# RWKV keys turned to time-major form by VectorE blocks and SBUF transfers instead of TensorE transposes

## The chip, the cores and the metric

The kernel runs on one core of one Trainium2 chip. The metric is device time in microseconds (us) of one execution, and lower is better. The time before is the median of 3 runs, 2657.88 us (2653.09 to 2657.88). Engines are named as the profile names them: PE (TensorE matmul), PEld (its weight loads), DVE (VectorE), ACT (ScalarE), POOL (GpSimd), SP (SyncE, which here only issues transfers).

## The reference

One decoder layer on 2048 tokens of width 1024: RMSNorm, one input projection, then two mixers side by side (HGRN2 with 4 heads of 128, RWKV-7 with 8 heads of 64), an output projection, and a ConvFFN. The part that this case touches is the RWKV-7 state:

```python
def step(S, inp):
    rt, wt, kt, vt, at, bt = inp
    sa = jnp.einsum('bhvk,bhk->bhv', S, at)
    S = S * wt[:, :, None, :] + sa[..., None] * bt[:, :, None, :] + vt[..., None] * kt[:, :, None, :]
    y = jnp.einsum('bhvk,bhk->bhv', S, rt)
    return S, y
```

The kernel computes it by chunks of 64 tokens. Within a chunk the dependence of the tokens on each other is a triangular system, solved on VectorE. What a chunk adds to the state is a sum over its 64 tokens of an outer product of `kt` (or `bt`) with a value row. On TensorE such a sum runs over partitions, so the keys must lie with time on the partitions, while the stage before makes them with the key channel on the partitions. Turning them is the work that the change moves.

## The kernel before

Phase 1 (to about 1327 us) holds the projections and both mixers; phase 2 (the rest) is the last output projection and the ConvFFN. Phase 1 is written as three generators: `dense` (the projection matmuls, lines 270 to 272, 8 steps of 3 matmuls for each column group), `rw_stream` and `hg_stream`. A loop takes one piece of each in turn and fills up with `dense` work. A scheduler then sets the order of each engine's instructions from that recorded program; each engine runs its own list strictly in order.

`rw_super` handles 512 tokens of four heads, and is run 8 times (8 stages below). Partitions hold two heads of 64 channels. Its steps, by line:

- L714 to L718: DVE writes `KB`, the scaled keys, [128 channels, 8 groups, 4, 64 tokens]. L730: PE multiplies `KB` with `AR` into score tiles; L733: DVE masks them into `M` (8 instructions of 128x512 a stage).
- L739 to L748: the 32x32 diagonal blocks of `M` go to DRAM (`Ed`, 4 transfers of 64 KB in runs of 128 bytes) and come back as `E` (2 transfers), with one system to a partition.
- L750 to L756: `KBT`, the keys with time on the partitions: 16 PE transposes of 128x128 into PSUM and 2 ACT copies of 128x1024. **This is what is changed.**
- L758 to L775: `RHS` and `UV`. `AT` is transposed (L763), `v` is centred and turned by a matmul (L768), ACT copies both out of PSUM; `UV` receives the values.
- L777 to L788: `lv`, matmuls that read `UV`; results go to `RHS`.
- L796 to L802: 31 elimination steps on DVE, two instructions each. L806 and L812: the result `TZ` is turned by DVE transposes in 32x32 blocks.
- L815 to L845: matmuls z, z2 and qus, which need `TZ` and `RHS`; L865 and L878: the state matmuls, the first readers of `KBT`.
- L897 to L937: the 8 chunk steps of the state, group norm, gate, and the store of the stage's output.

Buffers go by tags. `UV` shares its one buffer with `W` (the decay powers, dead by L716). `KBT` shares one with `ai`, and `RHS` takes the buffer of `KB`. PSUM tiles of `bank2()` have 2 buffers, so the two that the transposes take are handed from and to their neighbours.

All transfers of `rw_super` stand in SP's list; the weights of `dense` are fetched by POOL's list.

Of the kernel before, what the change touches and what calls it, by code (L numbers as in the profile page):

```python
# [11 lines left out]
AF = mybir.ActivationFunctionType  # L12
# [6 lines left out]
P = 128  # L19
# [48 lines left out]
def tile_layer(ctx, tc, consts, x, norm1_w, w_in, hg_lb_logits, hg_norm_w, rw_shift_mu, rw_w0, rw_w2,  # L68
# [4 lines left out]
    V, S, TE = nc.vector, nc.scalar, nc.tensor  # L73
    dma, store = nc.sync.dma_start, nc.gpsimd.dma_start
# [11 lines left out]
    ident = cp.tile([P, P], F32, name="ident")  # L86
# [27 lines left out]
    def act(out_, in_, func, **kw):  # L114

        want = tables.get(func)
        if want is not None and want != tab["now"]:
            pre = S.preload_act_table_set(want)
            for u_ in tab["uses"]:
                tc.add_manual_dep(pre.ins, u_.ins.name, NOSYNC, reason="table order")  # L120
            tab.update(now=want, pre=pre, uses=[])
        i_ = S.activation(out_, in_, func, **kw)  # L122
        if want is not None:
            tc.add_manual_dep(i_.ins, tab["pre"].ins.name, NOSYNC, reason="table order")
            tab["uses"].append(i_)
        return i_
# [13 lines left out]
    with tc.tile_pool(name="vp", bufs=1, reuse_waits="tile") as vp, tc.tile_pool(name="ps0", bufs=1, space=PSUM, reuse_waits="tile") as pools["ps"]:  # L140
        rows = vp.tile([P, P], F32, name="rows")
        V.memset(rows, 0.0)
        n = 0
# [130 lines left out]
    def phase1(c1):  # L274
# [372 lines left out]
        def rw_super(nb, s_):  # L647

            tl = stage[("tl", nb)]
            r, k, v = (stage.pop(("rkv", nb, s_, w)) for w in range(3))  # L650
# [3 lines left out]
            def tile_(tag, shape, name):  # L654
                return rp.tile([P] + shape, F32, tag=tag, name=name)

            def bank2():
                return ps.tile([P, 2, BLK], F32, tag="rw", name="rw", bufs=2)
# [5 lines left out]

            ai = tile_("KBT", [2, 2, BLK], "ai")
            a, iW = ai[:, 0], ai[:, 1]
# [9 lines left out]
            c, km, sq = mk_[:, 0], mk_[:, 1], mk_[:, 2]  # L676
# [37 lines left out]
            KB = tile_("KB", [8, 4, 64], "KB")  # L714
# [8 lines left out]
            for j in range(2):  # L723
                for u in U:
                    s1 = bank2()
                    for i in range(4):
                        b, e = 2 * j + i // 2, i % 2
# [20 lines left out]
                dma(E[f:P:2], Ed)  # L748

            KBT = tile_("KBT", [2, 8, P], "KBT")  # L750
            for u in U:
                tp = bank2()
                for i in range(8):
                    TE.transpose(tp[:, i // 4, (i % 4) * P:(i % 4 + 1) * P],
                                 KB[:, 4 * u + i // 2, (i % 2) * 2:(i % 2) * 2 + 2, :], ident)
                act(KBT[:, u], tp.rearrange("p j (c t) -> p (j c) t", t=P), AF.Copy)  # L756
            yield
            RHS = tile_("KB", [8, 2, P], "RHS")  # L758
            UV = tile_("UV", [8, 2, P], "UV")
            tp = bank2()  # L760
# [100 lines left out]
            for u in U:  # L861
                for ch in range(8):
                    b, e = ch // 2, ch % 2
                    for h in range(2):
                        TE.matmul(xp[h * 64:h * 64 + 64, u, ch * 64:ch * 64 + 64], KBT[:, u, ch, h * 64:h * 64 + 64],  # L865
                                  UV[:, 4 * u + b, e, h * 64:h * 64 + 64], start=ch == 0, stop=False,
                                  tile_position=(0, h * 64), skip_group_check=True)
            for u in U:
                Q, G = M[:, 0, u, :, :, 0:64], M[:, 1, u, :, :, 0:64]
                yg = bank2()  # L870
                for w in range(2):
                    for b in range(4):
                        for e in range(2):
                            rs_ = slice(er0(e), er0(e) + 64)
                            sl = w * 256 + b * 64
                            for h in range(2):
                                rhs = (M[rs_, e, u, b, h, 64:128] if w == 0
                                       else KBT[rs_, u, 2 * b + e, h * 64:h * 64 + 64])  # L878
                                TE.matmul(yg[h * 64:h * 64 + 64, e, sl:sl + 64], Q[rs_, b, h, :], rhs,
# [8 lines left out]
            for u in U:  # L888
                for ch in range(8):
                    b, e = ch // 2, ch % 2  # L890
# [6 lines left out]
            for ch in range(8):  # L897
                b, e = ch // 2, ch % 2
# [185 lines left out]
        def rw_stream():  # L1084
            for n in range(2 * NBLK):
                while ready["rw"] <= n:
                    yield None
                yield from rw_super(n // 2, n % 2)
# [53 lines left out]
    with ExitStack() as c2:  # L1142
# [36 lines left out]
        with tc.tile_pool(name="op", bufs=1, reuse_waits="tile") as op_:  # L1179
# [7 lines left out]
            b = NBLK - 1  # L1187
# [53 lines left out]
            for dh in range(2):  # L1241
                accs = [pst("wacc") for _ in range(4)]
                for n, k in enumerate((0, 1, 4, 5, 2, 3, 6, 7)):
# [22 lines left out]
                    for q in range(12):  # L1266
                        i, t_ = (q % 4, q // 4) if first else (q // 3, q % 3)
# [231 lines left out]
    with tc.tile_pool(name="dn", bufs=1, reuse_waits="tile") as dn:  # L1499
# [61 lines left out]
        for s_ in range(DS, N):  # L1561
            g, p, kk = steps[s_]
# [60 lines left out]
```

## Time and profile before

| what | value |
|---|---|
| median of 3 runs | 2657.88 us |
| the profiled execution's own time | 2662.58 us |
| its span, first to last instruction | 2660.8 us |
| granted TensorE clock over the span | 0.992 |
| PE / DVE / ACT / POOL busy | 2560.2 / 1952.9 / 1389.2 / 380.4 us |
| transfers | 510.59 MB, mean 192 GB/s |

The page gives busy time by engine, then a line of digits for each engine over 40 equal slices of the span (about 66.5 us each; 9 means 90% or more busy). Phase 1 is the first 20 slices. Windows are stretches of the span in which busy time is added up. A row of a line or a tile gives count and the shortest, median and longest duration in ns. A wait is an engine's idle time, put down to what ended it.

### The profile page before, as it was taken

The numbers are of one execution on the slowest core, as the hardware profiler recorded it, in microseconds if no ns is written. First come the engines' busy times: TensorE is split into PE (matmuls) and PEld (weight loads), VectorE is DVE, ScalarE is ACT, GpSimd is POOL, SyncE is SP. The second block draws the span as 40 slices with busy tenths as digits, with TensorE's granted clock in tenths as the row PEclk, the third lists the DMA queues.
The fourth block names the chain that finished last, engine by engine and source line by source line (L and its number), as shares of the span: only waits on it lengthen the run. The fifth ranks groups of instructions, "written<-read, shape, count | busy, mean of one in ns | idle before, by whom it ended". The sixth has DMA issues, their size and how long they took to land. (4 is left out here: it accounts for less than half of the span.)

```text
span 2660.8 us, 51050 instructions
## 1 busy us (share of the span) xinstructions
PE 2560.2 (96%) x19595; PEld 2061.2 (77%) x19595; DVE 1952.9 (73%) x3728; ACT 1389.2 (52%) x2274; POOL 380.4 (14%) x686
## 2 busy tenths in 40 slices
PE   7999999989999999999899999999999999999998
PEld 5777777766777777777678888887888887888887
DVE  4877667576567765767678789987998887766556
ACT  5566453545535555445456754456545544545444
POOL 6433222212222122222100000000000000000000
PEclk9999999999999999999999999999999999999999
DMA  8645443445643456744493468646763553998665
GB/s 303 204 165 170 158 143 120 130 148 203 199 143 126 156 196 199 276 131 136 154 309 113 143 204 266 233 154 225 245 203 131 166 189 127 327 320 286 197 191 186
DMA packets 312714, 510.59 MB, mean 192 GB/s; under 512 B 46879, under 2 KB 143509, under 8 KB 312469
## 3 DMA queue, kind: packets, MB, share of 16 engines
q1 hardware_dynamic: 257937, 328.99, 37.4%
q0 software_dynamic: 54464, 178.32, 20.4%
q8 instruction: 154, 2.52, 0.4%
q14 instruction: 91, 0.75, 0.1%
q10 hardware_dynamic: 68, 0.02, 0.0%
HBM read 372.99 MB, written 134.22 MB: 191 GB/s over the span
## 5 line engine op out<-in xcount | busy, mean ns | idle before, releaser
L270 PE MATMUL pj<-hh,wh 128*128 128x512 f32 x960 | 393.4, 410 | 6.2 <-ACT rkv L122 3.3
L271 PE MATMUL pj<-hl,wh 128*128 128x512 f32 x960 | 377.8, 394 | 1.3 <-issue 1.3
L272 PE MATMUL pj<-hh,wl 128*128 128x512 f32 x960 | 377.5, 393 | 0.0
L270 PE MATMUL ua<-Bh,uwh 128*128 128x512 f32 x704 | 276.4, 393 | 4.4 <-ACT m L122 3.1
L272 PE MATMUL ua<-Bh,uwl 128*128 128x512 f32 x704 | 274.6, 390 | 0.0
L271 PE MATMUL ua<-Bl,uwh 128*128 128x512 f32 x704 | 274.3, 390 | 0.0
L270 PEld LDWEIGHTS pj<-hh,wh 128*128 128x128 f32 x960 | 181.5, 189 | 55.2 <-issue 8.7
L272 PEld LDWEIGHTS pj<-hh,wl 128*128 128x128 f32 x960 | 181.1, 189 | 40.6 <-issue 1.7
L271 PEld LDWEIGHTS pj<-hl,wh 128*128 128x128 f32 x960 | 181.6, 189 | 34.3 <-DVE hl L488 0.5
L254 ACT CAST uwh<-uraw 128x512 fp32r<-128x512 f32 x220 | 134.2, 617 | 128.9 <-PE ua L271 55.7
L255 DVE TENSOR_TENSOR dal<-draw,dah 128x512 fp32r<-128x512 f32 x138 | 95.4, 691 | 113.4 <-ACT dah L254 113.2
L255 DVE TENSOR_TENSOR uwl<-uraw,uwh 128x512 fp32r<-128x512 f32 x220 | 147.6, 688 | 34.9 <-ACT uwh L254 34.8
L254 ACT CAST dah<-draw 128x512 fp32r<-128x512 f32 x138 | 85.7, 621 | 164.9 <-PE da L271 80.6
L270 PEld LDWEIGHTS ua<-Bh,uwh 128*128 128x128 f32 x704 | 132.2, 188 | 34.1 <-ACT m L122 5.7
L272 PEld LDWEIGHTS ua<-Bh,uwl 128*128 128x128 f32 x704 | 132.3, 188 | 28.1 <-DVE uwl L255 0.4
L271 PEld LDWEIGHTS ua<-Bl,uwh 128*128 128x128 f32 x704 | 132.3, 188 | 26.7
L270 PE MATMUL ud<-Bh,uwh 128*128 128x512 f32 x352 | 138.1, 392 | 0.0
L272 PE MATMUL ud<-Bh,uwl 128*128 128x512 f32 x352 | 137.2, 390 | 0.0
L271 PE MATMUL ud<-Bl,uwh 128*128 128x512 f32 x352 | 137.1, 390 | 0.0
L1493 POOL DMA_DIRECT2D gd<-y x2 | 1.1, 540 | 946.8 <-DVE y L1491 946.8
L271 PE MATMUL da<-dbl,dah 128*128 128x512 f32 x332 | 129.5, 390 | 0.2 <-DVE dbl L255 0.2
L272 PE MATMUL da<-dbh,dal 128*128 128x512 f32 x332 | 129.3, 389 | 0.0
(584 smaller groups left out, 6233.9 us busy)
## 6 DMA issues: line engine op xcount, KB each, us to landing
uraw<-in_w_up_dram SPq DMA_DIRECT2D x176, 256.0 KB, 3.1
woraw<-in_w_out_dram POOLq DMA_DIRECT2D x96, 256.0 KB, 3.6
br<-gd SPq DMA_DIRECT2D x88, 256.0 KB, 4.2
draw<-Sg SPq DMA_DIRECT2D x88, 256.0 KB, 3.3
draw<-Tw SPq DMA_DIRECT2D x88, 256.0 KB, 4.0
gd<-y SPq DMA_DIRECT2D x86, 256.0 KB, 2.9
Sg<-br SPq DMA_DIRECT2D x72, 256.0 KB, 2.1
xt<-x1d SPq DMA_DIRECT2D x32, 512.0 KB, 6.7
```

Source lines behind the costliest of these rows:

```text
L254: S.copy(hi, src)
L255: V.tensor_sub(lo, src, hi.bitcast(F32))
L270: TE.matmul(acc, lh, rh, start=first, stop=False, skip_group_check=skip)
L271: TE.matmul(acc, lh, rl, start=False, stop=False, skip_group_check=skip)
L272: TE.matmul(acc, ll, rh, start=False, stop=last, skip_group_check=skip)
L1493: (dma if end is None else nc.gpsimd.dma_start)(gd_[2 * h + b][fb * P:(fb + 1) * P, :], ys[0][:, b * BLK:(b + 1) * BLK])
```

## The change

The 16 PE transposes and 2 ACT copies of each stage become 2 DVE transposes and 16 transfers. DVE's transpose turns every 32x32 block of the keys in place: a block's 32 channels and 32 tokens change roles, but the four groups of 32 partitions stay where they are. The result goes to a new tile `KBb`, in which a free axis `a` still holds which quarter of the 128 tokens a block belongs to. Sixteen transfers (4 source groups `g` by 4 quarters `a`) then move each block to its partitions in `KBT`. Each moves 32 partitions x 16 runs of 32 floats, that is 512 runs of 128 bytes, 64 KB. `KBb` takes the tag of `UV`, so it lies in the buffer that `W` had before it and `UV` has after it. Nothing is left out of the computation.

```diff
             KBT = tile_("KBT", [2, 8, P], "KBT")
-            for u in U:
-                tp = bank2()
-                for i in range(8):
-                    TE.transpose(tp[:, i // 4, (i % 4) * P:(i % 4 + 1) * P],
-                                 KB[:, 4 * u + i // 2, (i % 2) * 2:(i % 2) * 2 + 2, :], ident)
-                act(KBT[:, u], tp.rearrange("p j (c t) -> p (j c) t", t=P), AF.Copy)
+            KBb = tile_("UV", [16, 4, 32], "KBb")
+            KBv = KBb.rearrange("p n a c -> p (n a) c")
+            for u in U:
+                V.transpose(KBv[:, 32 * u:32 * u + 32], KB[:, 4 * u:4 * u + 4].rearrange("p b k (a t) -> p (b k a) t", t=32))
+            for g in range(4):
+                for a in range(4):
+                    dma(KBT[32 * a:32 * a + 32].rearrange("p u i t -> p (u i) t")[:, :, 32 * g:32 * g + 32],
+                        KBb[32 * g:32 * g + 32, :, a, :])
             yield
```

The scheduler makes new lists of it. From line 758 on the new file's line numbers are two higher. Over the whole program PE has 128 instructions fewer, ACT 16 fewer, DVE 16 more and SP 128 more.

DVE's list, first stage, from the end of `KB` on (L255 is a split of projection weights, L945 to L972 are HGRN2 work; minus is before, plus is the change):

```order
 L718 TENSOR_TENSOR KB<-mk,ai 128x8x128
 L255 TENSOR_TENSOR wl<-wraw,wh 128x512 x2
-L945 TENSOR_SCALAR hk<-hf 128x512
-L963 TENSOR_TENSOR hX<-hq,hf 128x256
-L969 TENSOR_TENSOR hX<-hk,Sf 128x128x2
-L972 TENSOR_TENSOR hf<-hf 128x256
+L754 STREAM_TRANSPOSE KBb<-KB 128x1024
 L733 TENSOR_TENSOR M<-rw,cst 128x2x2x128 x2
-L963 TENSOR_TENSOR hX<-hq,hf 128x128x2
+L754 STREAM_TRANSPOSE KBb<-KB 128x1024
 L733 TENSOR_TENSOR M<-rw,cst 128x2x2x128 x2
```

The two transposes stand ahead of the mask products, and HGRN2 work that stood there has moved behind them.

SP's list, first two stages (`Ed` and `E` are the two ways of the diagonal blocks, `oT` the outputs of the two mixers, L1076 and L937 before, L1078 and L939 now):

```order
 L424 DMA xt<-in_x_dram 128x1024 x4
+L757 DMA KBT<-KBb 32x16x32 x4
 L745 DMA Ed<-M 32x16x32 x4
+L757 DMA KBT<-KBb 32x16x32 x2
 L748 DMA E<-Ed 64x1024 x2
-L1076 DMA oT_143<-osq 128x512
-L937 DMA oT_143<-yo 128x2x512
-L1076 DMA oT_143<-osq 128x512
+L757 DMA KBT<-KBb 32x16x32 x10
```

The 16 transfers stand partly ahead of `Ed`, two between `Ed` and `E`, and the rest behind `E`. Over the eight stages 3 to 8 of them stand ahead of `Ed`, and 6 to 11 behind `E`.

ACT's list, first stage, further on, in the change (`KT` and `Af` are HGRN2's, `RHS` is what `lv` gives):

```order
L122 ACTIVATE sgm<-pj 128x512
L122 ACTIVATE KT<-hg 128x512
L122 ACTIVATE Af<-hg 64x4x64
L122 ACTIVATE UV<-rw 64x8x128 x2
L254 CAST wh<-wraw 128x512
L122 ACTIVATE RHS<-rw 128x8x64
L122 ACTIVATE RHS<-rw 64x8x64 x2
```

Before, the two `UV` copies stood right behind the copies of `RHS` from the transposed `AT`, about a dozen rows earlier. On PE the `lv` matmuls move back likewise: between the `v` matmuls (L768) and `lv` stood 9 dense matmuls of 512 columns (12 in one stage), and now 63 to 102.

## The prediction

> **What bounds the kernel now.** I read the page first, then busy time by windows, then PE's waits.
>
> ```profile
> span 2660.8 us, 51050 instructions
> PE 2560.2 (96%) x19595; PEld 2061.2 (77%) x19595; DVE 1952.9 (73%) x3728; ACT 1389.2 (52%) x2274; POOL 380.4 (14%) x686
> DVE  4877667576567765767678789987998887766556
> ```
> ```profile
> 0.00:31.00 31.00, 15.41 (x64) 11.51 (x65) 15.00 (x37) 18.19 (x38) 18.48 (x36) 1.00 0.79 261
> 31.00:1327.00 1296.00, 1229.88 (x13735) 968.16 (x13733) 882.26 (x2098) 663.47 (x1097) 346.97 (x624) 0.99 0.52 171
> 1327.00:2660.80 1333.80, 1314.86 (x5798) 1081.54 (x5798) 1055.61 (x1595) 707.53 (x1141) 14.99 (x28) 1.00 0.64 211
> ```
>
> A windows row gives the stretch, its length, then busy time of PE, PEld, DVE, ACT and POOL, the granted clock, the transfers' share and GB/s. The change acts in the second row alone. There PE is busy 1229.9 of 1296 us, DVE 882, ACT 663. Phase 2's rows hold nothing of it, and its instructions stand in the same order. So PE's own work is the bound, and an instruction taken from PE is worth its slot as long as no wait takes its place. PE's longest waits in that stretch (total us, times, longest):
>
> ```profile
> PE rw L865 <- ACT M L122: 6.8, 7, 2.1
> PE pj L270 <- ACT hh L247: 6.4, 7, 1.4
> PE hg L1063 <- DVE SH L1055: 5.1, 3, 4.1
> PE hg L1042 <- DVE hk L1035: 5.0, 5, 1.6
> ```
>
> None is long. But DVE's average hides its stages. Here are the eight stretches from the end of `KB` to the last mask product; then, from there to the first elimination step, stage 1 and the sum over eight; then, from there to `TZ`, stage 5 and the sum.
>
> ```profile
> 84.60:95.80 11.20, 11.20 (x97) 9.07 (x96) 10.10 (x22) 2.47 (x5) 7.22 (x11) 1.00 0.83 264
> 225.00:237.80 12.80, 12.80 (x102) 10.48 (x103) 10.07 (x22) 2.68 (x6) 3.67 (x6) 1.00 0.39 130
> 367.30:377.80 10.50, 10.50 (x92) 8.62 (x91) 9.82 (x20) 1.04 (x2) 2.13 (x4) 1.00 0.47 151
> 506.80:520.90 14.10, 13.85 (x107) 11.21 (x106) 9.72 (x20) 1.54 (x3) 2.79 (x6) 1.00 0.24 76
> 711.50:720.70 9.20, 9.01 (x95) 7.49 (x95) 8.73 (x19) 5.44 (x10) 0.00 (x0) 1.00 0.67 253
> 849.10:862.30 13.20, 13.04 (x105) 10.59 (x104) 9.96 (x21) 2.87 (x6) 2.13 (x4) 1.00 0.27 81
> 1049.30:1058.00 8.70, 8.51 (x94) 7.17 (x94) 8.63 (x19) 5.30 (x10) 0.00 (x0) 1.00 0.64 238
> 1193.10:1204.30 11.20, 11.20 (x95) 9.21 (x94) 9.93 (x20) 0.94 (x2) 2.13 (x4) 1.00 0.43 139
> ```
> ```profile
> 95.80:107.50 11.70, 11.61 (x131) 10.06 (x129) 3.59 (x6) 9.79 (x13) 4.73 (x8) 1.00 0.82 236
> sum 93.40, PE 92.93 PEld 80.05 DVE 11.55 ACT 55.95 POOL 24.79; mean PE 11.62 PEld 10.01 DVE 1.44 ACT 6.99 POOL 3.10
> ```
> ```profile
> 733.60:759.80 26.20, 26.20 (x323) 21.50 (x323) 23.41 (x92) 8.57 (x19) 9.61 (x18) 1.00 0.62 205
> sum 252.50, PE 240.23 PEld 196.67 DVE 222.50 ACT 93.34 POOL 71.30; mean PE 30.03 PEld 24.58 DVE 27.81 ACT 11.67 POOL 8.91
> ```
>
> DVE is nearly full before the mask products, nearly empty while the diagonal blocks go to DRAM and back (11.6 of 93.4 us), and 88% busy in the elimination. What follows the elimination on PE is z:
>
> ```profile
>   DVE TZ L806: 5.8, 7
> ```
>
> PE waits for `TZ` before z 7 times, 5.8 us in all: it arrives at z 0.8 us before DVE is done. So PE's list and DVE's chain through the elimination run neck and neck, and DVE work put ahead of the elimination can cost PE time at z.
>
> **What is removed.**
>
> ```profile
> L754 PE MATMUL rw<-ident,KB x128: 270/273/300, 95.3 to 1208.9; 128*128 128x128 f32 x128
> 95.08 0.39 PE L272 MATMUL pj<-hh,wl 128*128 128x512 f32 x1
> 95.31 1.91 PE L754 MATMUL rw<-ident,KB 128*128 128x128 f32 x16
> 97.06 0.27 PE L950 MATMUL hg<-ident,hv 128*128 128x128 f32 x1
> L122 ACT ACTIVATE KBT<-rw x16: 1004/1021/1025, 96.4 to 1209.3; 128x1024 f32<-128x1024 f32 x16
> ```
>
> A transpose takes 273 ns, but they overlap: 16 start at 95.31 and the next matmul at 97.06, so a stage holds PE for 1.75 us (a dense matmul, in the same way, 95.08 to 95.31: 0.23). Eight stages: **-14.0 us on PE**. ACT loses 16 x 1.02 = 16.3 us; at 663 of 1296 us it is no bound, so I count 0 for it, and at the best 3 us, part of the 13.2 us of the two waits on ACT above.
>
> **What is added on DVE.** No row shows a transpose of 128x1024. The nearest:
>
> ```profile
> L806 DVE STREAM_TRANSPOSE TZ<-Ti x8: 961/1060/1103, 136.0 to 1247.5; 128x512 f32<-128x512 f32 x8
> L812 DVE STREAM_TRANSPOSE TTs<-TZ x32: 699/702/710, 137.3 to 1251.2; 32x512 f32<-32x512 f32 x32
> L718 DVE TENSOR_TENSOR KB<-mk,ai x8: 1217/1220/1225, 83.3 to 1191.9; 128x1024 f32<-128x1024 f32 x8
> ```
>
> L806 reads elements 16 apart, L812 pairs; the new one reads and writes without gaps. Twice L812 is 1.40 us, twice L806 2.12 us, an ordinary operation on as many columns 1.22 us. I take 1.3 us (bounds 1.22 and 2.12): 16 x 1.3 = 20.8 us more DVE work.
>
> Does it reach PE? First, up to the last mask product: pricing both lists by the trace's rows, the new one holds 0.4, 2.6, 2.6, 2.6, 2.2, 2.6, 1.7 and 2.6 us more DVE work there (where it is less than 2.6, HGRN2 work has moved behind). The idle time in the eight rows is 1.1, 2.7, 0.7, 4.4, 0.5, 3.2, 0.1 and 1.3 us; it is spent waiting for PE's score matmuls, so it can be filled. What is left makes the mask products late by 0, 0, 1.9, 0, 1.7, 0, 1.6 and 1.3 us. HGRN2 work moved behind them falls into the stretch where DVE is empty, and is free. From the first elimination step to `TZ` the new list has +1.3, -1.9, -2.0, +4.1, +0.4, +4.4, -5.8 and +1.0 us. On PE, from the first score matmul to z, dense matmuls have moved too; with the transposes gone PE gets to z later by 0.5, 0.1, -1.7, 2.3, -2.9, 4.3, -5.8 and 2.1 us. Lateness of `TZ` less lateness of PE: 0.8, -2.0, 1.6, 1.8, 5.0, 0, 1.6 and 0.2 us. The positive ones add to 11.0 us. Against them stands the elimination's own idle time, 252.5 - 222.5 = 30 us, mostly in stages 4, 6 and 7. Taken off stage by stage it leaves little but stage 5, which has 26.2 - 23.4 = 2.8 us of it and so pays 2.2. I take **+4 us** between 2 and 11, near the lower end because DVE's idle time there is real room. At 2.12 us for a transpose, 13 us more work would add up to 7.
>
> The Trainium skill speaks against the move: its page "VectorE: DVE Perf Modes", section "Rules for kernel authors", says to use TensorE for a 128x128 transpose if PSUM will do as the destination, and "The three transpose paths" there gives 390 ns on TensorE and 311 ns on VectorE for 128x128 in bf16. By its 390 ns a stage would free 6.2 us; the rows above show that transposes in a run cost PE 109 ns each, and this decides. By its 311 ns a transpose of eight such blocks would take 2.5 us, beyond my upper bound, and the sum would come to about no change.
>
> **What is added on the transfers.** The nearest rows are those of `Ed`, also runs of 128 bytes, 512 to a transfer, issued by SP. Two rows on the packets of the stretch 95 to 102 us, two on L745, then moments of stage 1:
>
> ```profile
> DMA packets 2519, 1.61 MB, mean 229 GB/s; under 512 B 2191, under 2 KB 2191, under 8 KB 2519
> q1 hardware_dynamic: 2112, 0.26, 28.0%
> L745 SPq DMA_DIRECT2D Ed<-M x32: 318/500/1177, 95.8 to 1205.8; - x32
> DMA to landing us min/median/max: 2.0/3.3/4.7
> ```
> ```profile
> 95.82 2.26 SPq L745 DMA_DIRECT2D Ed<-M  x4
> 101.91 1.12 SPq L748 DMA_DIRECT2D E<-Ed  x2
> 100.43 1.95 PE L768 MATMUL rw<-cst,rkv 128*128 128x128 f32 x16
> 107.56 0.19 DVE L800 TENSOR_TENSOR etmp<-E,Ti 128x31 f32<-128x31 f32 x1 [0.80 <-DMA E<-Ed]
> ```
>
> 28.0% of 16 engines x 7 us over 2112 packets is 14.8 ns a packet. A transfer of 512 is 0.47 us of all engines, 16 are 7.6 us a stage; SP issues them at 0.50 us each, 8 us a stage. So SP and the engines keep step, and no queue builds up. Of the 16, 3 to 8 stand ahead of `Ed`. They need only `KB` turned, which by the new list is done 6 us (stage 1) or 10 us (stage 2) before the last mask product, so SP sends them while it would wait. Two more stand between `Ed` and `E`: 1 us, and `E` waits for `Ed` to land anyway (95.82 + 2.26 to 101.91). So `E` is late by 0 to 1 us a stage; where DVE is the one that is waited for, this reaches z. I take **+1 us** in all, bounds 0 and 8.
>
> `UV` now waits for the last transfer. In stage 1 this is 101.91 + 1.12 + 10 x 0.5 + 3.3 = 111.3 us; the new list has 91 dense matmuls (0.23 us each) between the `v` matmuls, done at 102.4, and `lv`: 123 us. With 2 us for ACT's copies that is nine us of cover; if it were gone, PE would stop at `lv`, and ACT at `UV` with the casts of projection weights behind it.
>
> **The sum.** -14.0 + 4 + 1 = **-9 us**. From the profiled execution's 2662.58 us (span 2660.8 and 1.8 around it) to 2653.6; it lies 4.7 us above the median, so on the median 2657.88 - 9 = **2649 us**.
>
> **Rivals.**
>
> A, *DVE takes it all back*: the elimination's idle time is no room, all 11 us of lateness reach PE at z, and 1 to 4 us come from `E`. For it: PE waits for `TZ` in 7 of 8 stages already. Against: the 30 us of idle DVE. Time: -14 + 11 + 2 = -1, 2657 us.
>
> B, *slower: the transfers hold up `E`*. Place: the transfer engines between the last mask product and the first elimination step, a stretch that averages 11.7 us and in which nothing on DVE can start. If a run of 128 bytes between two places of SBUF costs twice the 14.8 ns, 8 transfers ahead of `Ed` take 7.6 us, still run when `Ed` is issued, and the two ahead of `E` add 1.9; projection weights, which share the engines, come late too. It decides from about 2 us of delay a stage. At 3 us: 8 x 3 = 24, -14 + 4 + 24 - 4 (stage 3 has room) = +10, 2668 us. For it: a stage's 7.6 us come where the engines are already 0.82 busy in stage 1; against: `Ed` landed in 3.3 us through the same load.
>
> On B's price, the Trainium skill's page "DMA: Bandwidth & Descriptors", section "Why small descriptors are slow (HBM only)", says that transfers within SBUF don't suffer from small pieces and reach 78% of the link with 128-byte packets. By this and the page's 435 GB/s, an estimate, a stage's 1 MB would take 3.1 us and not 7.6, and B would fall away; no row here has such a transfer.
>
> C, *the change doesn't free PE*: `lv` stops for `UV` in each stage, 2 us by 8 in place of the 14. The cover of nine us speaks against. -14 + 16 = +2, 2660 us.
>
> **How the numbers follow.** Forecast 0.50, A 0.27, B 0.18, C 0.05. Low end: all 14.0 and 3 from ACT, 2657.9 - 17 = 2641. High end: B's price, 2668, with about one in ten beyond. The forecast's own range is 2643 to 2652. A measurement can tell about 0.2%, 5.3 us, from no change. Faster by more: 0.52 (the forecast and a little of A); within: 0.29 (most of A, some of C); slower: 0.19.
>
> **What would show it.** Right: 128 PE instructions fewer, PE busy in phase 1 down by about 15 us; the new DVE rows near 1.3 us; PE's wait at z under 12 us; `E` landing within 13 us of the last mask product; no wait of PE at `lv`. Wrong: DVE rows near 2 us and PE waiting 15 us or more for `TZ` (A); the stretch to the first elimination step grown by 2 us or more a stage (B); a wait of ACT for `KBT`'s transfers before `UV` (C).

## The result, and the profile after

The changed kernel took **2648.7 us** (median of 14 runs, 2643.23 to 2657.38), the kernel before beside it 2657.99 us (14 runs, 2653.09 to 2667.32). The ratio is 0.9965, 95% interval 0.9953 to 0.9977: 0.35% or 9.3 us faster, where 9 were forecast. The profiled execution took 2645.42 us. Executions of one kernel spread over 14 us, so profiles are compared below by their rows, and kernels by their ratios. Much of the spread goes with PE's granted clock: among the 14 executions of the changed kernel it lies between 0.989 and 0.994, and by a straight line through them 0.001 less goes with 2.0 us more. One execution of the kernel with the DVE transposes alone (first experiment) took 3569.35 us in a slow state and is left out of its median.

The first lines of the changed kernel's page, then its row of the windows for phase 1, which now ends at 1310 us instead of 1327:

```profile
span 2643.6 us, 51054 instructions
...
PE 2547.0 (96%) x19467; PEld 2046.8 (77%) x19467; DVE 1963.7 (74%) x3744; ACT 1372.7 (52%) x2258; POOL 382.1 (14%) x686
```
```profile
31.00:1310.00 1279.00, 1214.72 (x13594) 953.02 (x13593) 889.90 (x2109) 644.24 (x1075) 347.77 (x622) 0.99 0.59 179
```

PE has 128 matmuls fewer, and its busy time in phase 1 fell from 1229.88 to 1214.72 us, by 15.2. Phase 2 is as long as it was (2643.6 - 1310.0 = 1333.6 us against 1333.8). The new work by the view of the tile `KBb` (its last row is the time from issue to landing), then SP's list in stage 1 by the timeline (start, length, count):

```profile
L757 SPq DMA_DIRECT2D KBT<-KBb x128: 591/640/2658, 89.3 to 1205.6; - x128
L754 DVE STREAM_TRANSPOSE KBb<-KB x16: 1192/1224/1243, 85.7 to 1184.9; 128x1024 f32<-128x1024 f32 x16
...
DMA to landing us min/median/max: 2.3/4.5/7.3
```
```profile
89.33 2.86 SPq L757 DMA_DIRECT2D KBT<-KBb  x4
96.70 2.10 SPq L745 DMA_DIRECT2D Ed<-M  x4
98.85 1.26 SPq L757 DMA_DIRECT2D KBT<-KBb  x2
100.73 1.16 SPq L748 DMA_DIRECT2D E<-Ed  x2
101.93 15.27 SPq L757 DMA_DIRECT2D KBT<-KBb  x10
```

A DVE transpose takes 1.22 us, the lower bound. SP's part is larger than forecast: the last ten transfers of stage 1 hold it for 15.27 us, and the issues of all stages add up to 105 us (0.82 us each in the mean, 11 to 19 us a stage) where 8 us a stage were forecast. In stage 1 the last of the 128-byte pieces ends at 120.8 us, where 111.3 was forecast. `UV`, which takes the buffer that the transfers read, comes late. Its first two copies in stage 1, by ACT's timeline, before and then in the changed kernel:

```profile
102.71 2.07 ACT L122 ACTIVATE UV<-rw 64x1024 f32<-64x1024 f32 x2
```
```profile
123.58 0.60 ACT L122 ACTIVATE KT<-hg 128x512 f32<-128x512 f32 x1
124.19 0.38 ACT L122 ACTIVATE Af<-hg 64x256 f32<-64x256 f32 x1
124.49 2.07 ACT L122 ACTIVATE UV<-rw 64x1024 f32<-64x1024 f32 x2
```

From the first issue of `Ed` to `UV` it is 102.7 - 95.8 = 6.9 us before and 124.5 - 96.7 = 27.8 us after; over the eight stages the traces give means of 9.5 and 26.9 us. No row in the changed kernel has ACT waiting for a transfer of `KBT`: the scheduler, which reckons with the transfers, has set `UV` that late in ACT's list, and `lv` in PE's. Nor does PE stop for it. Who waited for `UV` at `lv`, all stages (us, times):

```profile
  PEld rw L782: 2.7, 7
  PE rw L782: 0.3, 1
```

`E` comes later too: its median landing goes from 3.1 to 4.6 us, and from its first issue to the first elimination step the eight stages add up to 52.2 us before and 66.7 after, 1.8 us more a stage. PE's longest waits in phase 1, then the idle time of PE and PEld before z that `TZ` ended:

```profile
PE rw L867 <- ACT M L122: 9.7, 6, 3.6
PE pj L270 <- ACT hh L247: 6.0, 5, 2.0
PE hg L1084 <- DVE part L248: 4.4, 7, 1.8
PE rw L881 <- DVE AR L887: 4.3, 1, 4.3
...
PE rw L821 <- DVE TZ L808: 3.8, 4, 1.4
```
```profile
  DVE TZ L808: 9.7, 9
```

The 9.7 us, like the 5.8 of the forecast's row, are idle time of two engines in one sum. PE alone, before and then in the changed kernel:

```profile
  DVE TZ L806: 2.3, 3
```
```profile
  DVE TZ L808: 3.8, 4
```

So before the change PE waited for `TZ` 3 times, 2.3 us, and not 7 times, 5.8 us.

All of PE's waits in phase 1 add up to 64.0 us before and 64.1 after. So the gain is PE's work, and no wait went with it. That the medians lie 9.3 us apart and PE's busy time 15.2 may be the clock: the mean over the executions is 0.9911 for the changed kernel and 0.9931 for the kernel before (78 executions of it beside the experiments), and at 2.0 us for 0.001 the difference stands for about 4 us, an estimate. The experiments ask whether that is all there was to have.

### The profile page after: what moved, and what is told of

It is laid out like the page before. It is cut to its first block, busy times and chain, and to the rows that moved or that the text cites. A ratio compares the mean times of both kernels' runs of the same rounds, so it can differ in the third digit from the quotient of the medians.

```text
span 2643.6 us, 51054 instructions
## 1 busy us (share of the span) xinstructions
PE 2547.0 (96%) x19467; PEld 2046.8 (77%) x19467; DVE 1963.7 (74%) x3744; ACT 1372.7 (52%) x2258; POOL 382.1 (14%) x686
## 4 chain that ended last, share of the span: by engine, by line
PE 70%; DVE 11%; ACT 8%; DMA 7%; issue 3%; POOL 0%; SPq 0%; DVEq 0%; ACTq 0%; POOLq 0%
PE pj L270 7%; PE pj L271 7%; PE pj L272 6%; PE ua L270 5%; PE ua L272 5%; PE ua L271 5%; PE da L271 3%; PE da L272 3%; PE da L270 3%; PE ud L271 2%; PE ud L270 2%; PE ud L272 2%; PE db L272 2%; PE db L271 2%; PE db L270 2%
## 5 line engine op out<-in xcount | busy, mean ns | idle before, releaser
L255 DVE TENSOR_TENSOR dal<-draw,dah 128x512 fp32r<-128x512 f32 x138 | 95.2, 690 | 108.3 <-ACT dah L254 105.7
L255 DVE TENSOR_TENSOR uwl<-uraw,uwh 128x512 fp32r<-128x512 f32 x220 | 147.1, 684 | 34.3 <-ACT uwh L254 34.3
```

The lines of the kernel that those rows point to most:

```text
L255: V.tensor_sub(lo, src, hi.bitcast(F32))
```

## The experiments

Every ratio is to the kernel before, run beside it on the same chip. Line numbers differ by a few between kernels. The edits are shown against the changed kernel unless said otherwise.

**1. The change taken apart.** First the removal alone:

```diff
-            KBT = tile_("KBT", [2, 8, P], "KBT")
-            KBb = tile_("UV", [16, 4, 32], "KBb")
...
-                V.transpose(KBv[:, 32 * u:32 * u + 32], KB[:, 4 * u:4 * u + 4].rearrange("p b k (a t) -> p (b k a) t", t=32))
...
-                        KBb[32 * g:32 * g + 32, :, a, :])
+            KBT = Zk.unsqueeze(1).unsqueeze(1).broadcast_to([P, 2, 8, P])
```

The second kernel keeps `KBb` and the two lines of `V.transpose`. The third has the 16 transfers, from `W`:

```diff
+            KBd = tile_("KBT", [2, 8, P], "KBd")
...
+                    dma(KBd[32 * a:32 * a + 32].rearrange("p u i t -> p (u i) t")[:, :, 32 * g:32 * g + 32],
+                        W[32 * g:32 * g + 32, :, 8 * a:8 * a + 32])
```

> The removal alone: the 16 TensorE transposes and 2 ScalarE copies of a stage are gone and nothing takes their place; the state matmuls read a constant tile of zeros in the place of KBT, so the new keys' share of the state is left out of the computation. The theory on record (PE's slots are the gain, 14.0 us; VectorE's transposes cost 4, the transfers 1): about 2658 - 14 = 2644 us, 0.9947 of before, down to 2641 if ScalarE's relief pays too. Rival 'reshuffle' (the changed kernel is faster only because the scheduler laid the lists differently, PE's slots being worth little): within 5 us of before, 2653 to 2658.

> The removal and the two VectorE transposes of a stage (into KBb, which nobody reads), without the 16 transfers; the state matmuls read zeros, so the new keys' share of the state is left out. Against the removal alone this adds 16 x 1.22 us on VectorE. Theory: 4 us more than the removal alone (2648 us). Rival A (VectorE's elimination has no room): 11 us or more above it (2655 us).

> The removal and the 16 transfers of a stage, without the VectorE transposes: transfers of the same shape (32 partitions x 16 runs of 128 bytes) read the decay powers W, in the buffer that KBb would have, and go to KBT's buffer, which nobody reads; the state matmuls read zeros, so the new keys' share of the state is left out. UV's copies still wait for the last transfer. Theory: 1 us more than the removal alone (2645 us). Rival B (the transfers hold up E, and with it the elimination): 5 us or more above it (2649 us and up), with the wait of PE for TZ grown.

| kernel | median us | ratio, 95% interval |
|---|---|---|
| removal alone | 2638.69 | 0.9935 [0.9922, 0.9947] |
| removal and DVE transposes | 2637.48 | 0.9929 [0.9915, 0.9943] |
| removal and transfers | 2647.42 | 0.9963 [0.9952, 0.9975] |

The removal brings 17 to 19 us, not 14. The DVE transposes cost nothing that can be told. The transfers cost 7 to 9 us: nearly all that separates the changed kernel from the removal alone. `W`, from which they read here, has the buffer that `KBb` has in the changed kernel, so `UV` stands behind them here too. PE's waits in phase 1 are 66.7 us here and 52.6 with the removal alone. Rival B's sign, a longer wait for `TZ`, did not come: the idle time of PE and PEld that `TZ` ended is 4.9 us here. With the removal alone, then with the DVE transposes, it is

```profile
  DVE TZ L802: 10.6, 9
```
```profile
  DVE TZ L806: 10.3, 9
```

**2. PE's share and ACT's.** One removed part put back, its result unread: the 16 PE transposes, and in another kernel the two ACT copies.

```diff
+            for u in U:
+                tp = bank2()
+                for i in range(8):
+                    TE.transpose(tp[:, i // 4, (i % 4) * P:(i % 4 + 1) * P],
+                                 KB[:, 4 * u + i // 2, (i % 2) * 2:(i % 2) * 2 + 2, :], ident)
```
```diff
+            junk = tile_("XH", [8, P], "junk")
+            for u in U:
+                act(junk, KB[:, 4 * u:4 * u + 4].rearrange("p b k t -> p (b k t)").rearrange("p (i t) -> p i t", t=P), AF.Copy)
```

> The changed kernel, with the 16 TensorE transposes of a stage put back beside it: they go to the same PSUM tiles as before and nobody reads them; ScalarE's copies stay away. The result is the full one. Theory: PE's slots are worth their 1.75 us a stage, so 2649 + 14 = 2663 us. Rival 'reshuffle': 2649 to 2653 us.

> The changed kernel, with ScalarE's two copies of 128x1024 a stage put back (into a tile that nothing reads; they read KB and not PSUM). The removal alone brought 18.7 us, of which the PE slots, put back by themselves, account for 12.6. Theory 1, as predicted: ScalarE's 16.3 us are worth nothing; about 2649 us, within 1.5 us of the changed kernel. Theory 2: the rest of the gain, 4 to 6 us, is ScalarE's; about 2653 us, with longer waits of PE on M and on hh.

With the PE transposes 2661.3 us, ratio 1.0015 [1.0005, 1.0025], some 13 us above the changed kernel; with the ACT copies 2650.3 us, 0.9967 [0.9954, 0.998], which can't be told from it. In the first, PE's groups have the 128 transposes with 15.5 us of busy time, 0.12 us each, and no wait of note:

```profile
L762 PE MATMUL rw<-ident,KB 128*128 128x128 f32 x128 | 15.5, 273 | 0.4 <-DVE M L733 0.4
```

PE's slots are worth what the prediction said, and ACT's relief nothing. That the removal alone gave some 4 us more is left over. PE's waits in phase 1 are 52.6 us there, 11 less than before, but the intervals would allow the 4 us to be none.

**3. Is it the late `E`?** All 16 transfers behind `E` on SP.

```diff
-                dma(E[f:P:2], Ed)
+                e_in = dma(E[f:P:2], Ed)
...
-                    dma(KBT[32 * a:32 * a + 32].rearrange("p u i t -> p (u i) t")[:, :, 32 * g:32 * g + 32],
+                    k_in = dma(KBT[32 * a:32 * a + 32].rearrange("p u i t -> p (u i) t")[:, :, 32 * g:32 * g + 32],
...
+                    tc.add_manual_dep(k_in.ins, e_in.ins.name, NOSYNC, reason="E first")
```

> The changed kernel, with SP's order altered: none of a stage's 16 transfers of KBT may be issued before the two transfers of E. So far the 16 transfers alone cost about 8 us against the kernel without them (2647.4 to 2638.7 us). Theory E: they cost it because Ed and E, and with them the first elimination step, come late (rival B's mechanism at a smaller price). Then this kernel gets 5 to 8 us back, about 2642 us, the median landing of E falls from 4.6 us towards 3.1 us and the stretch from E's issue to the first elimination step returns to about 52 us over the eight stages (66.7 in the changed kernel). Theory UV: they cost it because UV waits for the last of them, so that lv and all behind it move. Then this kernel is no faster, 2649 to 2655 us, since the last transfer lands later still. Theory L: they cost it through the load on the engines wherever they stand: about 2649 us.

2646.09 us, 0.9948 [0.993, 0.9966]; the changed kernel's 0.9965 lies within. `E` does come on time (median landing 3.3 us, 52.4 us from issue to elimination over the stages), and `UV` later still, a mean of 38 us behind `Ed`. Theory E wanted 2642 us, theory UV 2649 or more; the time stands between them, and the run decides nothing.

**4. Is it the small pieces?** The same bytes in runs of 2 KB.

```diff
-            KBT = tile_("KBT", [2, 8, P], "KBT")
-            KBb = tile_("UV", [16, 4, 32], "KBb")
-            KBv = KBb.rearrange("p n a c -> p (n a) c")
+            KBT = tile_("KBT", [P, 16], "KBT")
+            KBb = tile_("UV", [4, 32, 16], "KBb")
+            KBv = KBb.rearrange("p a c n -> p n a c")
...
+                    dma(KBT[32 * a:32 * a + 32, 32 * g:32 * g + 32], KBb[32 * g:32 * g + 32, a])
...
-                                       else KBT[rs_, u, 2 * b + e, h * 64:h * 64 + 64])
+                                       else KBT[rs_, h * 64:h * 64 + 64, 8 * u + 2 * b + e])
```

> The changed kernel with the same bytes in 16 times fewer pieces: KBb is laid out [a, t, n] and KBT [time, 16 blocks], so that each of the 16 transfers moves 32 runs of 2 KB and not 512 of 128 bytes. For this VectorE writes its blocks with a stride of 16 elements, and the state matmuls read KBT's columns 16 elements apart. If the transfers cost by pieces (SP's 0.64 us an issue, 13 ns of an engine for 128 bytes), SP's issues shrink well below 0.5 us each, E lands in 3.1 us again, and 5 to 8 us come back: about 2641 us. If they cost by bytes, or because UV waits for them at all, about 2649 us. The price of the strides is unknown: L806's rows of before, strided, took 1.06 us for 512 columns, so up to 2.1 us a transpose and not 1.22, which two transposes a stage that were found to cost nothing at 1.22 us should bear within 5 us; PE's strided reads would show as a longer PE busy time in phase 1.

2671.3 us, 1.0047 [1.003, 1.0064]: 22 us slower than the changed kernel. The tile `KBT` in the changed kernel, then in this one; last, this one's `KBb`:

```profile
L867 PEld LDWEIGHTS rw<-UV,KBT x512: 132/138/227, 152.9 to 1254.2; 128*64 128x64 f32 x171
L867 PE MATMUL rw<-UV,KBT x512: 222/222/316, 152.9 to 1254.2; 128*64 128x64 f32 x171
...
L881 PE MATMUL rw<-KBT,M x512: 218/218/311, 157.4 to 1258.2; 64*64 64x64 f32 x171
```
```profile
L866 PEld LDWEIGHTS rw<-UV,KBT x512: 184/206/224, 154.1 to 1281.5; 128*64 128x64 f32 x171
L866 PE MATMUL rw<-UV,KBT x512: 271/276/327, 154.1 to 1281.6; 128*64 128x64 f32 x171
...
L880 PE MATMUL rw<-KBT,M x512: 266/284/308, 158.7 to 1286.6; 64*64 64x64 f32 x171
```
```profile
L757 SPq DMA_DIRECT2D KBT<-KBb x128: 507/589/1904, 91.4 to 1225.5; - x128
L754 DVE STREAM_TRANSPOSE KBb<-KB x16: 1878/1935/1953, 86.5 to 1211.4; 128x1024 f32<-128x1024 f32 x16
...
  ACT UV L122: 9.1, 3
...
DMA to landing us min/median/max: 2.0/3.8/5.6
```

The strides took their price, and on PE, where the expectation had put no number: operands read 16 elements apart make the matmuls 276 and 284 ns long instead of 222 and 218, and in the groups of PE lines L866 and L880 have 32.9 and 17.8 us of busy time where L867 and L881 had 20.3 and 10.9, 19.5 us more on the bound. That hides what longer pieces would bring in time. What they bring on the queue is to be read all the same: with 16 times fewer of them, the median issue fell from 0.64 to 0.59 us and the median landing from 4.5 to 3.8 us (though here 6 to 16 of a stage's transfers stand ahead of `Ed`, and not 3 to 8), and ACT waited for the transfers before `UV`, 9.1 us. The pages' rows of `q1`, the queue whose packets grew (packets, MB, share of the time of 16 engines), before, in the changed kernel and in this one:

```profile
q1 hardware_dynamic: 257937, 328.99, 37.4%
```
```profile
q1 hardware_dynamic: 325521, 337.38, 40.1%
```
```profile
q1 hardware_dynamic: 264081, 337.38, 38.4%
```

With the spans of 2660.8, 2643.6 and 2671.0 us the added 8.4 MB took about 1040 us of engine time in pieces of 128 bytes and about 490 in pieces of 2 KB. So the pieces do have a price on the engines; what they cost the kernel, this run can't tell.

**5. Is it the buffer?** The kernel of the removal and the transfers again, but they read the constants, which nothing overwrites:

```diff
-                        W[32 * g:32 * g + 32, :, 8 * a:8 * a + 32])
+                        cst[32 * g:32 * g + 32, 0:512].rearrange("p (n c) -> p n c", c=32))
```

> Removal and 16 transfers a stage, no DVE transposes, as in the kernel of 2647.4 us, but the transfers read 128-byte runs of the constants, a tile that nothing overwrites, in place of the tile whose buffer UV takes next. (The state matmuls read a tile of zeros here, so the new keys' share of the state is left out.) So SP issues the same 16 transfers and the engines move the same pieces, but UV has no transfer to wait for. Theory UV: the 8 us are gone, about 2639 to 2641 us. Theories E and L: nothing changes, about 2647 us, E's median landing still above 4 us.

2641.38 us, 0.994 [0.9921, 0.9959], where it had been 2647.42 us and 0.9963 [0.9952, 0.9975]. SP issues as much (103 us over the stages), and `E` lands late, by the view of its tile:

```profile
DMA to landing us min/median/max: 5.0/5.7/6.4
```

The load is there, and most of the price is not. So the full changed kernel, with two tags exchanged: `RHS` takes the buffer that holds `KBb`, and `UV` the one that `KB` leaves. The control is the same edit in the kernel before.

```diff
-            RHS = tile_("KB", [8, 2, P], "RHS")
-            UV = tile_("UV", [8, 2, P], "UV")
+            RHS = tile_("UV", [8, 2, P], "RHS")
+            UV = tile_("KB", [8, 2, P], "UV")
```

> The changed kernel with two buffers swapped: UV takes the buffer that KB leaves, RHS the one that KBb leaves, so that UV no longer waits for the 16 transfers; RHS does, and it is read only after the elimination. All instructions and transfers stay. Theory UV (the kernel with transfers that UV need not wait for took 2641.4 us, the one where it must 2647.4): 5 to 7 us come back, about 2642 us, ratio to the kernel before 0.993 to 0.995, although E still lands in 4 us or more. Theory E/L (SP's queue and the engines): about 2648.5 us as the changed kernel, ratio 0.9965. If what the removal without transfers showed (2638.7) was a lucky order of PE's list and no effect of waits, nothing ties this kernel to it either, and it lies anywhere from 2642 to 2651.

> The kernel before, with TensorE's transposes, and only the two buffers swapped. No transfer stands between KB and UV here, so no theory gives it a gain: ratio 1.000, within 0.002. If it gains 5 us as well, what the swap brings in the changed kernel has nothing to do with the transfers.

The changed kernel with the exchange: **2635.86 us**, 0.9911 [0.9895, 0.9927], 22 us faster than the kernel before and 13 us faster than the change. The control: 2659.03 us, 0.9999 [0.9988, 1.001]. Of the first, SP's timeline in stage 1, then ACT's, then PE's waits at the state products and at z:

```profile
99.69 1.26 SPq L757 DMA_DIRECT2D KBT<-KBb  x2
101.39 1.48 SPq L748 DMA_DIRECT2D E<-Ed  x2
102.92 13.04 SPq L757 DMA_DIRECT2D KBT<-KBb  x10
```
```profile
102.51 2.05 ACT L122 ACTIVATE UV<-rw 64x1024 f32<-64x1024 f32 x2 [2.90 <-PE rw L770]
...
125.77 3.26 ACT L122 ACTIVATE RHS<-rw 64x1024 f32<-64x1024 f32 x4
```
```profile
PE rw L867 <- ACT M L122: 6.2, 7, 2.1
...
PE rw L881 <- issue: 3.6, 1, 3.6
...
PE rw L821 <- DVE TZ L808: 1.3, 3, 0.7
```

SP is as full as in the changed kernel (101 us of issues), `E` nearly as late (64.9 us from issue to elimination over the stages), and the DVE transposes are there. Only `UV` is early again, a mean of 7 us behind `Ed`; `RHS` is late in its place, and it is read only behind the elimination. PE's waits in phase 1 are 55.3 us, not 64.1. By these two pairs of kernels the price of the transfers hung, for the most part, on who takes their buffer.

Not all of the 13 us need be the waits themselves. In the six executions of the exchange PE's granted clock is 0.994 to 0.998, in the fourteen of the changed kernel 0.989 to 0.994 (means 0.9955 and 0.9911); at 2.0 us for 0.001 this stands for about 9 us, an estimate. Two executions with a clock of 0.994, the profiled ones, took 2639.62 and 2645.42 us, 5.8 apart. Between the two kernels with transfers from `W` and from the constants the clock hardly differs (0.9929 and 0.9937), and they are 6 us apart. Where the clock goes, the changed kernel's trace shows. PE's timeline in stage 1, the windows row of the stretch, and the same matmuls in stage 2 (62 in that row):

```profile
152.92 3.85 PE L867 MATMUL rw<-UV,KBT 128*64 128x64 f32 x64 [3.56 <-ACT M L122]
```
```profile
153.60:157.00 3.40, 3.40 (x73) 3.28 (x72) 0.00 (x0) 1.59 (x3) 0.54 (x1) 0.50 0.14 52
```
```profile
299.77 2.05 PE L867 MATMUL rw<-UV,KBT 128*64 128x64 f32 x62
```

Right behind a wait of 3.56 us the clock stands at 0.50 for 3.4 us, and the matmuls take 3.85 us and not 2.05. Phase 1 of this trace has six such stretches of 3.4 or 6.8 us, 27 us together, each begun within 4.5 us of the start of a wait of PE (0.7 to 4.3 us long). So a wait can cost more than its own length. That the wait brings the low clock on fits these rows; no run was made to show it.

**6. The exchange with `E` first, and lateness alone.** One kernel has the edits of the third and the fifth experiment together. The other is the removal alone, with `UV` made late by a chain of eight small transfers:

```diff
                 dma(E[f:P:2], Ed)
+            late = tile_("UV", [8, 32], "late")
+            dma(late[0:32, 0], E[0:32, 0])
+            for i in range(7):
+                dma(late[0:32, (i + 1) % 8], late[0:32, i])
```

> The swap of the two buffers and E's transfers ahead of the 16 transfers together. Theory UV: the swap has taken all that the order could, about 2641 us. If E's lateness has a price of its own, 2 to 4 us less than with the swap alone, about 2638 to 2640 us, near the kernels without transfers.

> The removal alone (2638.7 us; no DVE transposes, none of the 16 transfers; the state matmuls read a tile of zeros, so the new keys' share of the state is left out), but UV made late by another cause: a chain of eight transfers of 4 KB a stage, each reading what the one before wrote, in the buffer that UV takes next, begins when E has landed. They are 64 runs of 128 bytes in two transfers' time at most, so they load neither engines nor SP's queue, and they stand behind E. By its list lv then stands before z with 32 dense matmuls between them in stage 1, as in the changed kernel (42), where the removal alone has 226. Theory UV, that a late UV alone costs (it takes lv's place in PE's list away from the stage's early part, and PE's waits return): 2644 to 2648 us, ratio 0.995 to 0.997, PE's waits in phase 1 back from 53 us to 60 or more. Rival: lateness of UV is harmless as long as PE finds other matmuls, and the cost was the load of the 16 transfers while UV's buffer is held: about 2639 us, ratio 0.9935.

The exchange with `E` first took 2653.17 us, 0.9977 [0.9966, 0.9988], 17 us more than the exchange alone, against every expectation. The transfers end later, so ACT's copies into `RHS` do (128.0 us in stage 1 and not 125.8), and they empty the PSUM tile whose bank z needs. Who waited for `RHS`, in this kernel alone:

```profile
  PEld rw L822: 5.8, 3
  PE rw L822: 4.9, 3
```

That is part of it; all of PE's waits in phase 1 are 67.3 us. The mean clock of its twelve executions is 0.9906, and 0.9955 for the exchange alone, which at 2.0 us for 0.001 would be about 10 of the 17 us, an estimate.

The chain took 2655.5 us, 0.9986 [0.9971, 1.0], 13 to 17 us above the removal alone and twice what theory UV had asked for. PE's waits in phase 1 are 63.3 us. `UV` starts a mean of 35 us behind `Ed`, and PE does stop at `lv`:

```profile
PE rw L780 <- ACT UV L122: 21.2, 7, 5.8
```

So the 16 transfers are not needed to make `UV`'s lateness dear. But the course is another than in the changed kernel, where PE hardly stopped there; and the kernel of the third experiment, whose `UV` is as late, lost much less. Lateness has no fixed price by the microsecond: it seems to depend on what the lists hold to cover it.

## Why the prediction was right

**The time was right by luck: two errors cancelled.** By the steps of the prediction:

- *What bounds the kernel.* PE's own work in phase 1 held: its busy time fell by 15.2 us, and the transposes put back cost 13 us.
- *Removal, -14.0.* The slots were priced rightly, and "ACT counted 0" held. With the removal alone 17 to 19 us were gained; the sum had no term for the 11 us by which PE's waits fell there.
- *DVE, 1.3 us a transpose and +4 of lateness.* A transpose is 1.22 us, and the lateness cost nothing that can be told: 2637.48 against 2638.69 us. The idle time before z that `TZ` ended did grow (9.7 us, 5.8 before, PE and PEld together), but not by DVE's transposes, for the first experiment has 10.6 us of it without them and 10.3 with them. That fits a PE that, freed of its own transposes, comes to z sooner. The step also rested on a misreading: "PE waits for `TZ` before z 7 times, 5.8 us" counts PEld in; PE alone waited 3 times, 2.3 us. By its "The three transpose paths", the Trainium skill's page "VectorE: DVE Perf Modes" would make it 2.5 us a transpose, an estimate (311 ns for each 128x128, eight of them, in bf16); the trace has 1.22 us and decides.
- *Transfers, +1.* **This is the term that was mis-sized: they cost 7 to 9 us.** "SP and the engines keep step, and no queue builds up" failed (15.27 us for ten issues where 5 were reckoned), and "`E` is late by 0 to 1 us a stage" is 1.8. Yet neither makes most of the price: the kernel with the exchanged tags has both and is the fastest of all. What failed is the pricing of `UV`'s wait. Its place was worked out well (`lv` at 123 us in stage 1; 125.9 measured), and of the nine us of cover some four were left there (the last piece ends at 120.8 us, the copies into `UV` begin at 124.5). But it was booked at nothing as long as PE didn't stop at `lv`, and the exchange, which moves `UV` back to 7 us behind `Ed`, brings 13 us.
- *The sum.* -14 + 4 + 1 = -9; the parts measured are about -18, 0 and +8, which make -10.

The rivals. A fell: DVE took nothing back, `TZ` held PE for less than the 12 us allowed, and the "7 of 8 stages" that spoke for A is the misread row. B rightly named the transfers, but at three times their price (24 us) and at the wrong place: `E` was late by close to the 2 us a stage from which B was to decide, and with the tags exchanged nearly the same lateness (64.9 us over the stages, not 66.7) did not keep the kernel from being the fastest. The rule cited beside B, from the Trainium skill's page "DMA: Bandwidth & Descriptors", section "Why small descriptors are slow (HBM only)", is not borne out here: the same bytes took twice the engine time in pieces of 128 bytes as in pieces of 2 KB. A stage's transfers took 1040 / 16 / 8 = 8.1 us of all engines, close to the 7.6 of the forecast and far from the 3.1 worked out from the page, whose 78% is measured on a remote transfer. B's own condition, twice the 14.8 ns a packet, did not come either. C named the right buffer, and the wrong form: PE's stop at `lv` was 0.3 us and PEld's 2.7, and ACT didn't wait for the transfers; what is left is the order that the scheduler made around the late `UV`.

What stays open is by which waits a late `UV` becomes 8 to 13 us. Between the changed kernel and the one with exchanged tags, PE's waits fall by 8.8 us in all: at `M` (9.7 to 6.2), at HGRN2's `part` (4.4 to 0.2), at `TZ` (3.8 to 1.3) and at L881 (4.3 put down to `AR` and 1.5 to "issue", then 3.6 to "issue"), while others grow. A lower clock behind waits may be part of the rest. In stage 1 the trace of the changed kernel has 50 dense and HGRN2 matmuls between the last of `lv` and the first of z, that of the kernel before 346 and that of the exchange 363. A reading that fits is that matmuls spent ahead of `lv` are missing as cover behind it. It is argued, not shown, and the kernel of the third experiment, with none there, speaks against a simple form of it. How far the 13 us are the mechanism and how far the luck of an order, these runs can't say: in the sixth experiment `UV` is early (a mean of 7.0 us behind `Ed`), `E` is on time, and another order still cost 17 us.

## What to carry to other kernels

When new transfers borrow a buffer, ask which tile takes it next and when that tile is first needed, and give the slow holder's buffer to the tile that is needed last; here two exchanged tags, with the same work in another order, were worth more than the change itself, though an order that looked as good lost it all again. A wait that other work covers need not be free where a scheduler has to move that work to cover it. Compare the granted clock of two kernels' executions before all of a difference is put down to one cause. And a forecast that comes out should still be taken apart: here a loss of 8 us and a gain of 8 us not foreseen had hidden each other.

## What the runs showed of the hardware

SP's time for one issue is not fixed: transfers of 512 runs of 128 bytes take 0.59 us at the shortest, 0.64 in the median and 1.5 us each in the ten of stage 1 (15.27 us), while `Ed`, with as many runs, had a median of 0.50 us before. fp32 operands that PE reads 16 elements apart are dear: 276 ns and not 222 for a matmul with such a stationary operand of 128x64, 206 and not 138 ns for its load, 284 and not 218 ns with a moving operand read so. A 128x1024 fp32 transpose on VectorE takes 1.22 us, and 1.94 us if it writes 16 elements apart. Transfers from SBUF to SBUF took about 1040 us of engine time for 8.4 MB in pieces of 128 bytes and about 490 in pieces of 2 KB. In the changed kernel's phase 1 PE's clock stood at 0.50 in six stretches of 3.4 or 6.8 us, each begun within 4.5 us of the start of a wait of PE.
